# Forget biases from the score products into a per-pair mask tile

## The chip, the cores and the metric

One Trainium2 chip, one core. The metric is the device time of one execution in microseconds, lower is better. The profiled execution has a time of its own, and its trace's span runs from the first to the last instruction.

## What is computed

Two layers over 512 tokens of width 1024 in float32. Each layer has eight forget heads and eight dilated heads of 64. A forget head is softmax attention with a bias from cumulated log forget gates:

```python
c = jnp.cumsum(log_f, axis=1).transpose(0, 2, 1)
s = jnp.einsum('bqhd,bkhd->bhqk', q_i, k) * scale
s = s + c_i[..., :, None] - c[:, :, None, :]
s = jnp.where(causal, s, NEG)
prob = jax.nn.softmax(s, axis=-1)
```

The term of the query, c_i, is the same for a whole row and drops out of the softmax; the kernel adds the term of the key only. After attention come a SiLU gate, an output projection, and a gated per-layer embedding.

## The kernel before

Heads are handled in pairs of two, 64 rows each: pairs 0 to 3 of a layer are dilated, pairs 4 to 7 forget. Values are split into a high and a low part (fp32r), and a product of two split operands is three products on TensorE (hi x hi, hi x lo, lo x hi).

One pass p = 1 to 7 of the loop at L743 projects pair p for four token tiles (pj, L690), evacuates each tile (ev, L695: squares on ScalarE, sum `ms` on VectorE, power -0.5 `f` on GpSimd at L445, scaling `z` on VectorE at L458), and in between does the attention of the pair a = p - 1 and the value product of p - 2. Pair 7 is scored after the loop, in between parts of the output projection. TensorE's order is that of the program; the order on VectorE, ScalarE, GpSimd and SyncE is made by a scheduler when the program is built, and each engine then runs its order strictly in turn.

The scores are in att_s (L572). For four query tiles qt of 128 (3 first) and both heads j, products go into PSUM tiles of (qt+1) x 128 columns (at least 256): three for the split query and key and, for a forget pair, a fourth, whose stationary operand `low` is all ones and whose moving operand CB holds the cumulated log gates (L583 to L590). Rows 0 and 1 of each 64-row half of CB are the high and low part of the gates of one head, all other rows are zero. Scores carry a minus sign: the scale is -0.125 (L345), so the smallest is sought, and the exponential has scale -1. Then for each tile one VectorE instruction adds a mask (`mask_fox` or `mask_dil`, both in the constant tile `cst`) and takes the row minimum `mx` (L597), ScalarE makes the exponential and its sum (L599), VectorE the reciprocal (L600), GpSimd the scaling (L601).

The gates are cumulated once in a layer, in pass 4 (cumulate, L502): products with a triangle in `tri`, then C2, high parts in rows 0 to 7, low parts in rows 32 to 39. bias_rows (L518) copies four rows of C2 to CB for a pair, with four transfers on ScalarE's queue; it is called in pass 4 for pair 4 and after att_s in passes 5, 6, 7 for the next pair.

The probabilities are transposed by TensorE (att_tp, att_tp2, L608 and L614), split into `PT` (ScalarE L621, VectorE L622), and multiplied with the values. Weights come over SyncE's queue as `raw` (L115) and are split into whi (ScalarE L157) and wlo (VectorE L158). The gate of a pair is L482 (VectorE) and L483 (tanh on ScalarE); QQ and KK are the split query and key (L548 to L557).

Of the kernel before, what the change touches and what calls it, by code (L numbers as in the profile page):

```python
# [9 lines left out]
F32 = mybir.dt.float32  # L10
F32R = mybir.dt.float32r
I32 = mybir.dt.int32
AF = mybir.ActivationFunctionType
# [4 lines left out]
P = 128  # L18
# [37 lines left out]
def constants():  # L56
    i = np.arange(P)[:, None]
    j = np.arange(P)[None, :]
    ident = (i == j).astype(np.float32)
    causal = np.where(j <= i, 0.0, BIG)  # L60
    mf = np.concatenate([np.zeros((P, 3 * P)), causal], axis=1)
    blocks = []
    for b in (3, 2, 1, 0):
        dist = b * P + i - j
        c = (dist <= 128).astype(int) + (dist % 4 == 0) + (dist % 16 == 0)
        c = np.where(dist >= 0, c, 0)
        blocks.append(np.where(c > 0, -np.log(np.maximum(c, 1)), BIG))
    md = np.concatenate(blocks, axis=1)
    return np.ascontiguousarray(
        np.concatenate([ident, mf, md], axis=1).astype(np.float32))  # L70


NCST = P + 2 * S

# [127 lines left out]
def trunk(tc, ap):  # L202
# [3 lines left out]
    with ctx:  # L206
# [39 lines left out]
        ident = cst[:, 0:P]  # L246
        mask_fox = cst[:, P:P + S]
        mask_dil = cst[:, P + S:P + 2 * S]
        tri = cp.tile([P, 5 * P], F32R, name="tri")
        lf = cp.tile([P, NT, 40], F32R, name="lf")  # L250
# [18 lines left out]
        KK = [cp.tile([P, S], F32R, name=f"KK{i}") for i in range(2)]  # L269
        CB = cp.tile([P, S], F32R, name="CB")  # L270
        PT = [cp.tile([P, 13, P], F32R, name=f"PT{i}") for i in range(2)]
        for l in range(DEPTH):
            W.own[("pt", l)] = (QQ, KK)
        C2 = cp.tile([40, S], F32R, name="C2")
        fx = cp.tile([P, NT, 8], F32, name="fx")
        hs = dp.tile([NK, P, S], F32, name="hs")

        ang = cp.tile([P, NT, 8], F32, name="ang")
# [39 lines left out]
        V.memset(ones1, 1.0)  # L318
        G.memset(CB.bitcast(F32), 0.0)
        for j in range(2):  # L320
            G.memset(PT[j][:, 0].bitcast(F32), 0.0)
        G.memset(tri[:, 0:P].bitcast(F32), 0.0)
        G.memset(tri[:, 2 * P:].bitcast(F32), 1.0)
        G.memset(lf.bitcast(F32), 0.0)
# [12 lines left out]
        def scale_columns():  # L337
            V.scalar_tensor_tensor(tri[:, P:2 * P], mask_fox[:, 3 * P:], 1.0, ident, op0=ALU.min,
                                   op1=ALU.add)
# [162 lines left out]
        def cumulate():  # L502
# [3 lines left out]
            for t in range(NT):  # L506
                n = max(NT - t, 2) * P
                T.matmul(ps[0:40, S - n:], lf[:, t], tri[:, P:P + n] if t < 3 else tri[:, :n],
                         start=(t == 0), stop=(t == NT - 1))
            c = tp.tile([8, S], F32, tag="ob", name="c")  # L510
            A.activation(c, ps[32:40], AF.Copy)
            V.tensor_tensor(c, ps[0:8], c, op=ALU.add)
            A.activation(C2[0:8], c, AF.Copy)
            V.tensor_tensor(C2[32:40], c, C2[0:8].bitcast(F32), op=ALU.subtract)

        HALF = (slice(0, 64), slice(64, P))

        def bias_rows(a):  # L518

            for j in range(2):  # L520
                h = 2 * (a - NDIL) + j
                for i in range(2):
                    A.dma_start(CB[64 * j + i:64 * j + i + 1].bitcast(F32),  # L523
                                C2[32 * i + h:32 * i + h + 1].bitcast(F32))

# [46 lines left out]
        def att_s(a):  # L572
            fox = a >= NDIL
            mask = mask_fox if fox else mask_dil
            low = tri[:, 2 * P:3 * P]
            b3, b2, pm = pair(psS, "psS"), pair(psS, "psS"), pair(psM, "psM")
            tiles = {}
            for qt in (3, 2, 1, 0):
                n = (qt + 1) * P
                nt = max(qt + 1, 2)  # L580
                for j in range(2):
                    tiles[(j, qt)] = (pm[j][:, 256:], pm[j][:, :256], b2[j][:, :384], b3[j])[qt]
                for i, (x, y) in enumerate(((0, 0), (0, 1), (1, 0), (2, 2))[:4 if fox else 3]):  # L583
                    for j in range(2):
                        if x == 2:
                            lhs, rhs = low[HALF[j]], CB[HALF[j], :nt * P]
                        else:
                            lhs = QQ[x][HALF[j], qt * P:(qt + 1) * P]
                            rhs = keys(KK[y], j, nt)
                        T.matmul(tiles[(j, qt)], lhs, rhs, start=i == 0, stop=i == 2 + fox)  # L590
            for qt in (3, 2, 1, 0):
                n = (qt + 1) * P
                for j in range(2):
                    seg = pseg(j, qt)
                    mx = sp.tile([P, 1], F32, tag="mx", name="mx", bufs=8)
                    sm = sp.tile([P, 1], F32, tag="sm", name="sm", bufs=8)
                    V.tensor_tensor_reduce(seg, tiles[(j, qt)][:, :n], mask[:, S - n:], 1.0, 3e38,  # L597
                                           ALU.add, ALU.min, mx)
# [85 lines left out]
        for l in range(DEPTH):  # L684
# [58 lines left out]
            for p in range(1, NPAIR):  # L743
# [24 lines left out]
                if p > 1:  # L768
                    with behind("A", "V"):
                        W.pump()  # L770
                pj(p, 2)
                ev(p, 2)
# [35 lines left out]
            part(1, 3, 5)  # L808
            att_o(b, oo)
            att_s(a)  # L810
            PT1 = [x.rearrange("p k s -> p (k s)")[:, :13 * P].rearrange("p (a b) -> p a b", a=13)
# [155 lines left out]
```

## Time and profile before

| | |
|---|---|
| median of three runs | 712.31 us (711.62 to 1372.89) |
| profiled execution | 712.22 us, span 710.4 us |
| TensorE, matmul busy | 699.4 us, 98% |
| TensorE, weight loads busy | 618.4 us, 87% |
| VectorE busy | 501.8 us, 71% |
| ScalarE busy | 382.3 us, 54% |
| GpSimd busy | 182.9 us, 26% |
| granted clock of TensorE | 0.999 |
| read from HBM | 60.49 MB |

PE is TensorE, PEld its weight loads, DVE VectorE, ACT ScalarE, POOL GpSimd, SP SyncE. Times in rows are microseconds from the span's start unless marked ns. A bracket at a row's end says how long the engine sat idle ahead of it, and what ended that. L12 is a line of the kernel before. One run of the three took 1372.89 us; it plays no part below.

### The profile page before, as it was taken

The page shows a single profiled execution, that of the slowest core. Times are in us where ns is not written, and L with a number is a line of the kernel's source. Part 1 is how long each engine was busy: PE and PEld are TensorE (multiplying, and loading weights), DVE is VectorE, ACT ScalarE, POOL GpSimd, SP SyncE. Part 2 cuts the span into 40 slices and gives each one's busy share as a digit, 9 for nine tenths or more (in the row PEclk, how much of TensorE's full clock was granted, in tenths as well). Part 3 has the DMA queues.
Part 4 walks back from the last instruction along what each step waited for, and adds up shares of the span by engine and source line. Part 5 has one row for each costly group of instructions (what it writes and reads, how often), then busy time and mean ns, then how long its engine had stood idle before and what let it go on. Part 6 is the DMA issues. An engine that isn't in the chain of part 4 may idle for free.

```text
span 710.4 us, 12211 instructions
## 1 busy us (share of the span) xinstructions
PE 699.4 (98%) x4424; PEld 618.4 (87%) x4424; DVE 501.8 (71%) x1240; ACT 382.3 (54%) x809; POOL 182.9 (26%) x326
## 2 busy tenths in 40 slices
PE   9999999999999999999999999999999999999997
PEld 8999898989989878888899899998889897888886
DVE  7887787766767677838738687777767767694633
ACT  8575556555555756525425556555654656582310
POOL 7462643313131320000004533614131240200000
PEclk9999999999999999999999999999999999999999
DMA  8612131221212145424423022222222113353211
GB/s 289 194 32 68 57 99 50 86 68 54 90 57 88 36 139 150 157 83 156 139 69 119 8 90 60 84 67 70 73 65 86 60 61 119 105 163 118 89 44 45
DMA packets 23948, 65.53 MB, mean 92 GB/s; under 512 B 4817, under 2 KB 6097, under 8 KB 23889
## 3 DMA queue, kind: packets, MB, share of 16 engines
q1 hardware_dynamic: 22576, 64.68, 28.6%
q8 instruction: 35, 0.57, 0.3%
q10 hardware_dynamic: 1312, 0.08, 0.1%
q14 instruction: 25, 0.20, 0.1%
HBM read 60.49 MB, written 4.19 MB: 91 GB/s over the span
## 4 chain that ended last, share of the span: by engine, by line
PE 64%; DVE 17%; ACT 8%; issue 4%; POOL 4%; ACTq 2%; DMA 0%; POOLq 0%; DVEq 0%
PE psA L88 42%; PE psS L88 16%; DVE wlo L158 5%; PE psM L88 4%; POOL f L445 3%; DVE PT L622 3%; ACT U L599 3%; ACTq L523 2%; ACT PT L621 1%; DVE U L597 1%; DVE U L653 1%; ACT whi L157 1%; ACT sqh L483 1%; DVE V L452 1%; DVE ms L442 1%
## 5 line engine op out<-in xcount | busy, mean ns | idle before, releaser
L157 ACT ACTIVATE whi<-raw 128x1024 fp32r<-128x1024 f32 (+3 forms) x105 | 106.7, 1021 | 68.2 <-PE psA L88 51.7
L158 DVE TENSOR_TENSOR wlo<-raw,whi 128x1024 fp32r<-128x1024 f32 (+3 forms) x105 | 122.8, 1171 | 13.3 <-ACT whi L157 13.2
L88 PE MATMUL psA<-whi,X 128*128 128x384 f32 (+1 forms) x480 | 130.5, 341 | 0.0
L88 PE MATMUL psA<-whi,Y 128*128 128x384 f32 (+1 forms) x480 | 129.3, 341 | 0.2 <-DVE U L482 0.2
L445 POOL TENSOR_TENSOR f<-ms,mhalf 128x4 f32<-128x4 f32 x64 | 64.7, 1012 | 243.7 <-DVE ms L443 234.1
L88 PE MATMUL psA<-Y,whi 128*128 128x512 f32 (+1 forms) x320 | 96.6, 385 | 0.7 <-DVE sqh L863 0.5
L88 PE MATMUL psA<-X,whi 128*128 128x512 f32 x304 | 95.7, 396 | 0.0
L599 ACT ACTIVATE U<-U,mx 128x512 f32<-128x512 f32 (+3 forms) x128 | 70.6, 553 | 39.4 <-DVE mx L597 34.5
L88 PEld LDWEIGHTS psA<-whi,X 128*128 128x128 f32 x480 | 87.9, 188 | 1.8 <-ACT whi L157 0.5
L88 PEld LDWEIGHTS psA<-whi,Y 128*128 128x128 f32 x480 | 87.5, 188 | 1.4 <-issue 0.4
L88 PE MATMUL psA<-wlo,X 128*128 128x384 f32 (+1 forms) x240 | 81.8, 341 | 1.7 <-DVE wlo L158 1.7
L88 PE MATMUL psA<-wlo,Y 128*128 128x384 f32 (+1 forms) x240 | 81.3, 339 | 1.2 <-DVE wlo L158 1.2
L601 POOL TENSOR_SCALAR U<-U,sm 128x512 f32<-128x512 f32 (+3 forms) x128 | 65.8, 534 | 55.0 <-DVE sm L600 54.2
L88 PEld LDWEIGHTS psA<-Y,whi 128*128 128x128 f32 x320 | 58.4, 188 | 13.5 <-DVE sqh L863 1.2
L88 PEld LDWEIGHTS psA<-X,whi 128*128 128x128 f32 x304 | 56.5, 188 | 13.1 <-DVE sqh L863 0.4
L88 PE MATMUL psA<-Y,wlo 128*128 128x512 f32 (+1 forms) x160 | 61.3, 383 | 0.0
L88 PE MATMUL psA<-X,wlo 128*128 128x512 f32 x152 | 59.9, 394 | 0.0
L458 DVE TENSOR_TENSOR z<-psA,f 128x256 f32<-128x256 f32 x60 | 25.4, 423 | 45.9 <-POOL f L445 45.9
L622 DVE TENSOR_TENSOR PT<-psS,PT 128x512 fp32r<-128x512 f32 (+1 forms) x58 | 37.1, 673 | 19.1 <-ACT PT L621 19.1
L440 ACT ACTIVATE sq<-psA 128x256 f32<-128x256 f32 x56 | 21.3, 381 | 53.4 <-PE psA L88 45.8
L88 PEld LDWEIGHTS psA<-wlo,X 128*128 128x128 f32 x240 | 45.2, 188 | 3.2 <-DVE wlo L158 3.2
L88 PEld LDWEIGHTS psA<-wlo,Y 128*128 128x128 f32 x240 | 45.1, 188 | 2.0 <-DVE wlo L158 2.0
(190 smaller groups left out, 1232.5 us busy)
## 6 DMA issues: line engine op xcount, KB each, us to landing
raw<-in_wq_dram SPq DMA_DIRECT2D x28, 576.0 KB, 3.9
raw<-in_wg_dram SPq DMA_DIRECT2D x16, 512.0 KB, 3.4
raw<-in_wo_dram SPq DMA_DIRECT2D x16, 512.0 KB, 3.4
raw<-in_wpg_dram SPq DMA_DIRECT2D x16, 512.0 KB, 3.4
raw<-in_wq_dram SPq DMA_DIRECT2D x14, 384.0 KB, 3.3
U<-in_xT_dram SPq DMA_DIRECT2D x16, 256.0 KB, 3.9
raw<-in_wple_dram SPq DMA_DIRECT2D x4, 512.0 KB, 3.6
hs<-U SPq DMA_DIRECT2D x8, 256.0 KB, 3.2
```

What stands on the lines that cost most here:

```text
L88: return self.tc.keep_in_program_order(self.eng.matmul(*a, **k))
L157: self.nc.scalar.activation(hi, r, AF.Copy)
L158: eng.tensor_tensor(lo, r, hi.bitcast(F32), op=ALU.subtract)
L440: A.activation(sq, ps[:, :2 * P].rearrange("p (h d) -> p h d", h=4), AF.Square)
L442: V.tensor_reduce(ms, sq, axis=AX.X, op=ALU.add)
L445: G.tensor_tensor(f, ms, mhalf.to_broadcast([P, 4]), op=ALU.pow)
L452: V.scalar_tensor_tensor(v2[:, t, :, HD:P], vps, st["r"][:, t:t + 1], v2[:, t, :, 0:HD].bitcast(F32), op0=ALU.mult, op1=ALU.subtract)
L458: last["V"] = V.tensor_tensor(z, ps[:, :2 * P].rearrange("p (h d) -> p h d", h=4), f[:, :, None].to_broadcast([P, 4, HD]), op=ALU.mult)
L523: A.dma_start(CB[64 * j + i:64 * j + i + 1].bitcast(F32), C2[32 * i + h:32 * i + h + 1].bitcast(F32))
L599: A.activation(seg, seg, AF.Exp, bias=mx, scale=-1.0, accum_out=sm)
L601: G.tensor_scalar(seg, seg, sm, 1.0, op0=ALU.mult, op1=ALU.mult)
L622: last["V"] = V.tensor_tensor(lo, src, hi.bitcast(F32), op=ALU.subtract)
```

## The change

The fourth product goes, with `low`, CB and C2. In their place stands MF, a tile of 20 blocks of 128 x 128 in float32: for head j and query tile qt the blocks that fox_mask names hold what L597 adds. cumulate writes the cumulated gates c (8 heads x 512) to HBM (`cd`). For a pair, bias_rows issues eight transfers on SyncE's queue, each of which reads the first (qt+1) x 128 gates of one head from `cd` and writes them to all 128 partitions of MF. bias_causal adds the causal block to the diagonal blocks of one head in one VectorE instruction of 128 x 4 x 128, so twice for a pair. The constant tile holds one causal block in place of four blocks, and `tri` loses its block of zeros.

```diff
@@ constants
-    mf = np.concatenate([np.zeros((P, 3 * P)), causal], axis=1)
-        np.concatenate([ident, mf, md], axis=1).astype(np.float32))
-NCST = P + 2 * S
+        np.concatenate([ident, causal, md], axis=1).astype(np.float32))
+NCST = 2 * P + S
@@ trunk
-        mask_fox = cst[:, P:P + S]
-        mask_dil = cst[:, P + S:P + 2 * S]
-        tri = cp.tile([P, 5 * P], F32R, name="tri")
+        causal = cst[:, P:2 * P]
+        mask_dil = cst[:, 2 * P:]
+        tri = cp.tile([P, 4 * P], F32R, name="tri")
-        CB = cp.tile([P, S], F32R, name="CB")
+        MF = cp.tile([P, 20, P], F32, name="MF")
-        C2 = cp.tile([40, S], F32R, name="C2")
+        cd = dp.tile([8, S], F32, name="cd")
@@ cumulate
-                n = max(NT - t, 2) * P
-                T.matmul(ps[0:40, S - n:], lf[:, t], tri[:, P:P + n] if t < 3 else tri[:, :n],
-                         start=(t == 0), stop=(t == NT - 1))
+                n = (NT - t) * P
+                T.matmul(ps[0:40, S - n:], lf[:, t], tri[:, :n], start=(t == 0),
+                         stop=(t == NT - 1))
             c = tp.tile([8, S], F32, tag="ob", name="c")
             A.activation(c, ps[32:40], AF.Copy)
             V.tensor_tensor(c, ps[0:8], c, op=ALU.add)
-            A.activation(C2[0:8], c, AF.Copy)
-            V.tensor_tensor(C2[32:40], c, C2[0:8].bitcast(F32), op=ALU.subtract)
+            nc.sync.dma_start(cd, c)
@@ bias_rows
+        def fox_mask(j, qt):
+            x0 = 7 + 3 * qt if j == 0 else 12 - 4 * qt
+            return MF[:, x0:x0 + qt + 1].rearrange("p a b -> p (a b)")
+
         def bias_rows(a):
-            for j in range(2):
-                h = 2 * (a - NDIL) + j
-                for i in range(2):
-                    A.dma_start(CB[64 * j + i:64 * j + i + 1].bitcast(F32),
-                                C2[32 * i + h:32 * i + h + 1].bitcast(F32))
+            for qt in range(NT):
+                for j in range(2):
+                    h = 2 * (a - NDIL) + j
+                    n = (qt + 1) * P
+                    nc.sync.dma_start(fox_mask(j, qt), cd[h:h + 1, :n].to_broadcast([P, n]))
+
+        def bias_causal():
+            for x in (MF[:, 7:20:4], MF[:, 3:13:3]):
+                V.tensor_tensor(x, x, causal[:, None, :].to_broadcast([P, NT, P]), op=ALU.add)
@@ att_s
-                for i, (x, y) in enumerate(((0, 0), (0, 1), (1, 0), (2, 2))[:4 if fox else 3]):
+                for i, (x, y) in enumerate(((0, 0), (0, 1), (1, 0))):
                     for j in range(2):
-                        if x == 2:
-                            lhs, rhs = low[HALF[j]], CB[HALF[j], :nt * P]
-                        else:
-                            lhs = QQ[x][HALF[j], qt * P:(qt + 1) * P]
-                            rhs = keys(KK[y], j, nt)
-                        T.matmul(tiles[(j, qt)], lhs, rhs, start=i == 0, stop=i == 2 + fox)
+                        T.matmul(tiles[(j, qt)], QQ[x][HALF[j], qt * P:(qt + 1) * P],
+                                 keys(KK[y], j, nt), start=i == 0, stop=i == 2)
-                    V.tensor_tensor_reduce(seg, tiles[(j, qt)][:, :n], mask[:, S - n:], 1.0, 3e38,
+                    mask = fox_mask(j, qt) if fox else mask_dil[:, S - n:]
+                    V.tensor_tensor_reduce(seg, tiles[(j, qt)][:, :n], mask, 1.0, 3e38,
                                            ALU.add, ALU.min, mx)
@@ pass p, ahead of pj(p, 2)
+                if a >= NDIL:
+                    bias_causal()
@@ after the loop
             att_o(b, oo)
+            bias_causal()
             att_s(a)
```

The scheduler places what the program asks for elsewhere than the text does. In pass 5 of each layer, VectorE comes to the two additions for pair 4 behind KK: one ahead of two halves of PT, one between the sum of squares `ms` and its scaling. The additions for pairs 5, 6 and 7 it sets a good deal earlier than the program's text, right behind the attention of the pair before. VectorE's order at the end of att_s for pair 4, in pass 5, in the kernel before (L600 is the last reciprocals, L442, L452 and L443 the evacuation of the pass's last token tile, L158 a weight split, L482 the gate):

```order
L597 ISA U_92,mx<-psM,cst 128x128
L597 ISA mx 128x1
L600 RECIPROCAL sm<-sm 128x1 x4
L442 TENSOR_REDUCE ms<-sq 128x4
L452 SCALAR_TENSOR_TENSOR V_116<-psA,r,V_116 128x2x64
L443 TENSOR_SCALAR ms<-ms,E 128x4
L458 TENSOR_TENSOR z<-psA,f 128x256
L158 TENSOR_TENSOR wlo<-raw,whi 128x1152
L482 TENSOR_TENSOR U_94<-psA,Rh 128x512
```

and in the changed kernel, whose own line numbers its rows carry (L529 is the addition, L439, L449, L440, L455, L157 and L479 are L442, L452, L443, L458, L158 and L482 of before):

```order
L597 ISA U_92,mx<-psM,MF 128x128
L597 ISA mx 128x1
L600 RECIPROCAL sm<-sm 128x1 x4
L529 TENSOR_TENSOR MF<-MF,cst 128x4x128
L439 TENSOR_REDUCE ms<-sq 128x4
L449 SCALAR_TENSOR_TENSOR V_116<-psA,r,V_116 128x2x64
L440 TENSOR_SCALAR ms<-ms,E 128x4
L529 TENSOR_TENSOR MF<-MF,cst 128x4x128
L455 TENSOR_TENSOR z<-psA,f 128x256
L157 TENSOR_TENSOR wlo<-raw,whi 128x1152
L479 TENSOR_TENSOR U_94<-psA,Rh 128x512
```

The two additions for pair 5 now stand inside the evacuation of the last token tile, the first ahead of its reduction, the second ahead of its z. It is the same in passes 6 and 7.

VectorE's order where att_s of pair 4 begins, before (the first four rows evacuate token tile 2):

```order
L442 TENSOR_REDUCE ms<-sq 128x4
L452 SCALAR_TENSOR_TENSOR V_116<-psA,r,V_116 128x2x64
L443 TENSOR_SCALAR ms<-ms,E 128x4
L458 TENSOR_TENSOR z<-psA,f 128x256
L597 ISA U_88,mx<-psS,cst 128x512
L597 ISA mx 128x1
L597 ISA U_91,mx<-psS,cst 128x512
```

and in the changed kernel:

```order
L439 TENSOR_REDUCE ms<-sq 128x4
L449 SCALAR_TENSOR_TENSOR V_116<-psA,r,V_116 128x2x64
L440 TENSOR_SCALAR ms<-ms,E 128x4
L597 ISA U_88,mx<-psS,MF 128x512
L597 ISA mx 128x1
L455 TENSOR_TENSOR z<-psA,f 128x256
L597 ISA U_91,mx<-psS,MF 128x512
```

The first mask reduction has moved ahead of z.

SyncE's order from the transfer of c to the weights of pass 6 in the changed kernel (L510 writes `cd`, L525 is a transfer into MF, L114 a weight load; before, only the weight loads stood there):

```order
L114 DMA raw<-in_wq_dram 128x1152
L510 DMA cd<-c 8x512
L525 DMA MF<-cd 128x128 x2
L525 DMA MF<-cd 128x256 x2
L525 DMA MF<-cd 128x384 x2
L525 DMA MF<-cd 128x512 x2
L114 DMA raw<-in_wq_dram 128x1152
L114 DMA raw<-in_wq_dram 128x768
L114 DMA raw<-in_wg_dram 128x1024
L525 DMA MF<-cd 128x512 x2
L525 DMA MF<-cd 128x384 x2
L525 DMA MF<-cd 128x256
```

Each later group of eight has the widest first, and stands behind the gate's weights of its pass and ahead of the loads of the next.

## Rows read from the trace of the kernel before

**Rows 1.** Windows, one per step: length, busy time (instructions) by engine, clock, DMA
```profile
147.23:178.49 31.26, 30.68 (x222) 27.88 (x222) 21.59 (x59) 17.81 (x42) 8.15 (x12) 1.00 0.24 68
178.49:209.47 30.98, 30.59 (x221) 28.05 (x220) 22.52 (x61) 17.39 (x41) 8.15 (x12) 1.00 0.23 70
209.47:240.09 30.62, 30.42 (x222) 28.02 (x222) 21.56 (x58) 17.24 (x41) 8.36 (x14) 1.00 0.21 70
406.76:436.32 29.56, 29.56 (x213) 27.44 (x213) 22.60 (x64) 17.40 (x41) 13.96 (x24) 1.00 0.23 72
496.02:527.37 31.35, 30.77 (x222) 27.90 (x222) 21.37 (x58) 17.87 (x42) 8.15 (x12) 1.00 0.23 69
527.37:558.62 31.25, 30.72 (x221) 28.11 (x220) 22.74 (x61) 17.40 (x41) 8.16 (x13) 1.00 0.23 68
558.62:589.33 30.71, 30.48 (x221) 28.06 (x220) 22.24 (x60) 17.22 (x41) 8.44 (x14) 1.00 0.22 70
```

**Rows 2.** Timeline of TensorE (start, length, instruction): score blocks, forget and dilated
```profile
196.70 0.97 PE L88 MATMUL psS<-KK,QQ 64*128 64x512 f32 x6
...
199.48 0.45 PE L88 MATMUL psA<-whi,X 128*128 128x384 f32 x1
...
424.19 1.50 PE L88 MATMUL psS<-KK,QQ 64*128 64x512 f32 x12
...
426.33 0.44 PE L88 MATMUL psA<-whi,Y 128*128 128x384 f32 x1
```

**Rows 3.** Timeline: transfers and tanh in pass 4, a wait of TensorE in pass 6
```profile
147.44 2.52 ACTq L523 DMA_DIRECT2D CB<-C  x4
...
150.01 0.63 ACT L483 ACTIVATE sqh<-U 128x512 f32<-128x512 f32 x1 [2.60 <-issue]
...
185.94 0.44 PE L88 MATMUL psA<-wlo,X 128*128 128x384 f32 x1 [0.39 <-DVE wlo L158]
```

**Rows 4.** The page's part 4, the chain that ended last, by engine
```profile
PE 64%; DVE 17%; ACT 8%; issue 4%; POOL 4%; ACTq 2%; DMA 0%; POOLq 0%; DVEq 0%
```

**Rows 5.** Timeline of one forget step, VectorE, ScalarE and its queue
```profile
200.02 0.68 DVE L597 CUSTOM_DVE_ANT_0 U<-psS,cst 128x512 f32<-128x512 f32 x1
...
203.97 0.28 DVE L597 CUSTOM_DVE_ANT_0 U<-psM,cst 128x128 f32<-128x128 f32 x1
...
205.22 0.55 ACTq L523 DMA_DIRECT2D CB<-C  x1
...
205.81 0.60 ACTq L523 DMA_DIRECT2D CB<-C  x1
206.51 0.39 ACT L440 ACTIVATE sq<-psA 128x256 f32<-128x256 f32 x1 [0.99 <-ACT U L599]
206.93 0.42 DVE L442 TENSOR_REDUCE ms<-sq 128x4 f32<-128x256 f32 x1 [1.21 <-ACT sq L440]
...
208.94 0.42 DVE L458 TENSOR_TENSOR z<-psA,f 128x256 f32<-128x256 f32 x1 [1.20 <-POOL f L445]
```

**Rows 6.** Lines, shapes apart: a 128x512 addition on VectorE
```profile
L387 DVE TENSOR_TENSOR acc<-acc,sqh 128x512 f32<-128x512 f32 x28 | 19.3, 688 | 0.0
```

**Rows 7.** Timeline of a dilated step: VectorE's addition beside GpSimd
```profile
423.25 1.35 DVE L158 TENSOR_TENSOR wlo<-raw,whi 128x1152 fp32r<-128x1152 f32 x1
423.42 1.29 POOL L463 TENSOR_TENSOR tm<-z,Sg 128x32 f32<-128x32 f32 x1 [0.54 <-DVE z L458]
...
427.68 0.25 POOL L463 TENSOR_TENSOR tm<-z,Sg 128x32 f32<-128x32 f32 x1 [0.54 <-DVE z L458]
```

**Rows 8.** DMA issues: out<-in queue xcount, KB each, median us to landing
```profile
CB<-C ACTq DMA_DIRECT2D x32, 2.0 KB, 1.7
out_dram<-U SPq DMA_DIRECT2D x2, 128.0 KB, 1.7
gr<-in_qkg_dram SPq DMA_DIRECT2D x2, 16.0 KB, 3.9
```

**Rows 9.** Timeline of ScalarE in pass 7 of layer 0
```profile
237.78 0.38 ACT L440 ACTIVATE sq<-psA 128x256 f32<-128x256 f32 x1 [1.71 <-issue]
```

More of the change, by code (lines that the diff above doesn't have):

```diff
@@ L318, in trunk @@
         V.memset(ones1, 1.0)
-        G.memset(CB.bitcast(F32), 0.0)
         for j in range(2):
             G.memset(PT[j][:, 0].bitcast(F32), 0.0)
-        G.memset(tri[:, 0:P].bitcast(F32), 0.0)
-        G.memset(tri[:, 2 * P:].bitcast(F32), 1.0)
+        G.memset(tri[:, P:].bitcast(F32), 1.0)
         G.memset(lf.bitcast(F32), 0.0)
@@ L337, in scale_columns @@
         def scale_columns():
-            V.scalar_tensor_tensor(tri[:, P:2 * P], mask_fox[:, 3 * P:], 1.0, ident, op0=ALU.min,
+            V.scalar_tensor_tensor(tri[:, 0:P], causal, 1.0, ident, op0=ALU.min,
                                    op1=ALU.add)
@@ L573, in att_s @@
             fox = a >= NDIL
-            mask = mask_fox if fox else mask_dil
-            low = tri[:, 2 * P:3 * P]
             b3, b2, pm = pair(psS, "psS"), pair(psS, "psS"), pair(psM, "psM")
```

## The prediction

> **What bounds the kernel now.** I read the steps first. A step runs from one pass's first block of transposes on TensorE to the next pass's. In [rows 1] a step whose scores belong to a dilated pair takes 29.56 us with TensorE busy throughout: such a step is TensorE-bound. The six steps that compute forget scores (three in each layer) take 30.62 to 31.35 us, 186.17 in all, against 6 x 29.56 = 177.36 at the dilated pace: 8.81 us more. The reader is to see that TensorE is busy for less than those spans.
>
> The fourth product explains part of it. The score block of a forget pair lasts from 196.70 to 199.48, 2.78 us; that of a dilated pair from 424.19 to 426.33, 2.14 us [rows 2]. So the product costs 0.64 us of TensorE per pair, 3.84 us in the six steps, and 1.28 us in the two pairs scored after the last pass, 5.12 us in all. The remaining 8.81 - 3.84 = 4.97 us of the six steps is TensorE waiting; [rows 3] end with one such wait, at 185.94, for a weight half (wlo) that VectorE makes late.
>
> Why VectorE is late is in the chain of waits, of which only 64% lies on TensorE [rows 4], and in the timeline of one step [rows 5]. The three products of its first block end at 196.70 + 0.97 = 197.67 [rows 2], but the first mask reduction starts at 200.02, because it stands in VectorE's order behind z, which waits for GpSimd's pow as the next z does at 208.94. Then follow eight reductions and eight exponentials; ScalarE, behind the last exponential, issues two transfers (0.55 and 0.60 us); the square comes at 206.51, its reduction on VectorE at 206.93, then GpSimd's pow, and z at 208.94. From there the weight split, the gate and the transposed probabilities follow without slack until the wait of [rows 3]. **The fourth product is not on this chain**: its end is covered by z. A forget step is as long as the chain, and taking work from TensorE alone lengthens TensorE's wait. What the change does to the chain therefore decides.
>
> **The change part by part.** The sum is made against the profiled execution's 712.2 us (span 710.4); the median of the runs shown is 712.31, so the two can be read as one.
>
> Fourth product: -0.64 us of TensorE per pair. In the six steps I count nothing for it by itself, since the chain hides it; with the cover gone it is worth the whole 0.64. After the last pass TensorE works through output-projection parts while the probabilities are made, so there it counts between 0 and 0.64; I take 0.6 per layer, nearer TensorE's side as the parts leave it little idle.
>
> First forget pass (p = 4) of each layer: the two casts of C2 and four transfers leave ScalarE. The transfers take ScalarE 2.52 us from 147.44 on, and the gate's tanh waits 2.60 us for them [rows 3]. What that step loses beyond product and pace is 31.26 - 29.56 - 0.64 = 1.06 us, the most that can come back. Against it stand two additions on VectorE in pass 5, each as long as a 128x512 addition, 0.69 us [rows 6]: one ahead of the second half of PT, which has room, one between two instructions that GpSimd's pow waits for. The new chain c to HBM and back (eight transfers behind one another on SyncE) starts at about 147.4, and ahead of the first addition VectorE has eight instructions of about the size of [rows 6], 8 x 0.69 = 5.5 us of work: room for two landings one after the other of under 3 us each. I take -0.7 per layer, between 0 and -1.06.
>
> Passes 5, 6, 7 of each layer, six times. Four things change on the chain of [rows 5]:
> (a) Two late transfers leave ScalarE: the square could follow the last exponential, about 1.1 us sooner (0.55 + 0.60; 205.4 in place of 206.51).
> (b) The first mask reduction now stands ahead of z and uses VectorE's wait for pow: the later seven come some 0.7 us sooner, and so do the exponentials.
> (c) The first addition for the next pair now stands right behind the last reciprocal and ahead of the reduction of squares. It waits for four transfers into MF, and those can be issued only when this pair's reductions have read MF. The last of the four follows the seventh reduction, which ended at 203.97 + 0.28 = 204.25 and by (b) ends near 203.5. With a time to landing of L the addition starts at 203.5 + L and the reduction of squares behind it at 203.5 + L + 0.69, against 206.93 now. Everything in VectorE's queue behind it (reduction, V, ms, z, the weight split, the gate) waits with it.
> (d) The second addition starts just ahead of GpSimd's pow. In [rows 7] a GpSimd operation of 0.25 us that meets a VectorE addition of two SBUF operands takes 1.29 us, until that addition ends. The pow itself was never met so (bounds: 0 and the 0.69 of the addition); I take 0.55, since the row that shows such a meeting shows a full wait.
> The shift of z is then 203.5 + L + 0.69 - 206.93 + 0.55 = L - 2.2 us.
>
> L is not shown for this transfer (one HBM row of 512 to 2048 bytes copied to 128 partitions). The nearest rows [rows 8]: 1.7 us for 2 KB and for 128 KB, and 3.9 us for a row broadcast to 128 partitions (gr) in the crowded first microseconds. The last transfer that counts is 64 KB and the queue is otherwise idle then, so I take 2.0, near the lower end: shift -0.2 us, with ends -0.5 (L = 1.7) and +1.7 (L = 3.9). Times six: -1.2, between -3.0 and +10.2.
>
> One term stands alone: in layer 0, pass 7, the transfers held the square back to 237.78, a wait of 1.71 us, not 0.99 [rows 5, 9]. That falls away: -0.7, once.
>
> Nothing is charged for bytes: 8 x 1.3 MB more is read, beside weight loads that are issued in good time. SyncE's order puts the eight transfers ahead of weight loads that are issued a step later anyway. In layer 0 the instructions of log_forget also come a little earlier in VectorE's and ScalarE's orders, in passes 1 and 2; TensorE does not depend on them before pass 4, and I count nothing.
>
> Sum: 2 x (-0.7 - 0.6) - 1.2 - 0.7 = -4.5 us; 712.2 - 4.5 = **707.7 us**.
>
> Two rules of the Trainium skill bear on (c) and (d), and the sum does without them. [Rows 7] show GpSimd held to the end of a VectorE addition; the page SBUF — State Buffer (SBUF: two separate sides) calls the port that VectorE's second SBUF input shares with GpSimd an exclusive lock, held for a whole instruction. By that rule (d) costs its 0.55, as charged; without it the sum would be 3.3 us lower, 704.4. [Rows 8] show what a wait right behind an issue costs here; the page DMA: Bandwidth & Descriptors (Rules for kernel authors) says to issue early, compute, and wait late. The order in (c) does the opposite of that, which is the second rival below.
>
> **The rivals.**
> 1. *TensorE becomes the bound of the forget steps too*: landing and pow hide, the chain gets shorter by (a) and (b), 1.8 us, less one addition, enough to cover TensorE's waits. Then all of 8.81 + 1.28 = 10.1 us comes back: 702.1 us. For it: TensorE is busy 98% and its waits are short. Against it: for 8.81 / 6 = 1.47 us per step, L - 2.2 has to fall to -1.47, which with (d) free still wants an L of 1.3 us, and no row shows one.
> 2. *The MF transfers land late, slower than before*: VectorE's in-order queue stands at the first addition in passes 5 to 7. The total of 2 x (-0.7 - 0.6) - 0.7 + 6 x (L - 2.2) passes zero at L = 2.75 us; at gr's 3.9 us it is +6.9: 719.1 us. For it: gr is the only row of this shape, and all 128 readers want one HBM row. Against it: gr lands in the crowded first microseconds, the MF transfers on an idle queue.
> 3. *The wait only changes its owner*: shift of z about 0.2 to 0.7 us, gains and new waits cancel: 710.1 to 713 us.
>
> **How the numbers follow.** Forecast (L of 1.7 to 2.4 and (d) of 0.2 to 0.55: 703.8 to 710.1 us): 0.5. Rival 1 (701 to 703.8): 0.13. Rival 3: 0.17. Rival 2: 0.2, of which 0.03 lies beyond 2%. The range that leaves out no more than 2 in 10 goes from 702 to 717; the forecast's own is 703.8 to 710.1. A measurement of this kernel can tell about 2%, 14 us, from no change. The floor of rival 1 is 1.4% below the present, so faster by over 2% gets 0.01; slower by over 2% needs L of about 5.1 us (14.2 + 3.3 = 17.5 us over six steps is a shift of 2.9), 0.03; within 2% 0.96.
>
> **What would show it.** Right: forget steps of about 30.3 to 30.6 us in passes 5 to 7, TensorE still waiting there for wlo, VectorE idle ahead of the first addition until MF lands, about 2 us after issue; the tanh of pass 4 no longer held. If the steps come down to 29.6 us, rival 1 holds. If the first addition starts after 207 on the scale of [rows 5], rival 2. If the pow behind the second addition takes 1.0 us with no delay, (d) is wrong. The forecast is wrong if dilated steps change by more than 0.1 us, for then something other than these waits moved.

## The result and the profile after

The changed kernel takes 729.29 us (median of four runs, 728.95 to 730.33) against 712.12 us of the kernel before on the same chip: ratio 1.0246, 95% interval 1.0226 to 1.0266. It is slower, and outside the range of 702 to 717. One run of the kernel before, 1372.89 us, counts in that median and is left out of the ratio.

The page's first lines of the changed kernel, busy time (share of the span) xinstructions, and the chain that ended last:

```profile
span 727.0 us, 12149 instructions
PE 701.6 (97%) x4360; PEld 621.2 (85%) x4360; DVE 509.3 (70%) x1254; ACT 379.6 (52%) x807; POOL 183.6 (25%) x324
...
PE 68%; DVE 14%; DMA 7%; POOL 4%; ACT 3%; issue 3%; SPq 1%; DVEq 0%; POOLq 0%; ACTq 0%
```

Against [rows 4], ScalarE and its queue have a smaller part of the chain (8% and 2% are now 3% and 0%) and DMA has come in with 7%. TensorE has 64 products fewer and yet is busy 2 us longer. The windows by step, as in [rows 1], the dilated step first, show where the time lies:

```profile
413.83:443.39 29.56, 29.56 (x213) 27.44 (x212) 22.61 (x64) 17.39 (x41) 13.97 (x24) 1.00 0.23 72
146.73:181.37 34.64, 31.32 (x214) 29.03 (x214) 22.61 (x61) 17.38 (x41) 7.39 (x12) 0.95 0.42 138
181.37:213.04 31.67, 30.26 (x213) 27.55 (x213) 22.38 (x59) 17.16 (x41) 8.20 (x12) 1.00 0.36 109
213.04:246.49 33.45, 31.51 (x214) 29.07 (x214) 23.98 (x65) 17.07 (x41) 8.89 (x15) 0.95 0.33 103
503.10:539.04 35.94, 32.22 (x213) 29.84 (x213) 22.32 (x61) 17.38 (x41) 7.21 (x12) 0.91 0.47 132
539.04:570.56 31.52, 30.13 (x214) 27.57 (x214) 23.12 (x60) 17.16 (x41) 8.07 (x12) 1.00 0.42 110
570.56:602.93 32.37, 30.28 (x214) 27.55 (x214) 22.24 (x60) 16.94 (x41) 8.74 (x14) 1.00 0.34 106
```

That dilated step is unchanged at 29.56 us. The first forget step of each layer is the worst (34.64 and 35.94 us, 31.26 and 31.35 before), and in three steps the granted clock is under 1.00, which it was in none before. The stretches behind the third forget steps, in which pair 7 is scored, are longer too: 23.64 and 25.25 us (246.49 to 270.13 and 602.93 to 628.18), 22.99 and 22.18 before. One dilated step is shorter, the first of layer 0: 29.51 us (56.66 to 86.17), 30.06 before. What VectorE waited for, in the view of waits (total, times, longest):

```profile
DVE MF L529 <- DMA MF<-cd: 27.1, 9, 4.8
...
PE psS L87 <- DVE PT L622: 7.3, 3, 3.7
PE psA L87 <- DVE U L479: 5.9, 6, 1.0
PE psM L90 <- DVE z L455: 3.5, 4, 1.6
```

The additions (L529) wait 27.1 us for transfers into MF, and TensorE then waits for what stands behind them in VectorE's order: the probabilities PT, the gate U, z. Two of the nine waits are for pair 4 (4.35 and 4.75 us); the others are for pairs 5 to 7. The timeline of VectorE in the step that [rows 5] showed, last reductions to z:

```profile
206.88 0.29 DVE L597 CUSTOM_DVE_ANT_0 U<-psM,MF 128x128 f32<-128x128 f32 x1
...
207.16 0.27 DVE L597 CUSTOM_DVE_ANT_0 U<-psM,MF 128x128 f32<-128x128 f32 x1
...
208.82 0.16 DVE L600 RECIPROCAL sm<-sm 128x1 f32<-128x1 f32 x1 [0.22 <-ACT U L599]
212.14 0.69 DVE L529 TENSOR_TENSOR MF<-MF,cst 128x512 f32<-128x512 f32 x1 [3.16 <-DMA MF<-cd]
212.75 0.41 DVE L439 TENSOR_REDUCE ms<-sq 128x4 f32<-128x256 f32 x1
...
213.47 0.69 DVE L529 TENSOR_TENSOR MF<-MF,cst 128x512 f32<-128x512 f32 x1
215.06 0.42 DVE L455 TENSOR_TENSOR z<-psA,f 128x256 f32<-128x256 f32 x1 [0.91 <-POOL f L442]
```

and of ScalarE, GpSimd, SyncE's queue and TensorE beside it:

```profile
208.69 0.36 ACT L437 ACTIVATE sq<-psA 128x256 f32<-128x256 f32 x1
...
213.71 1.32 POOL L442 TENSOR_TENSOR f<-ms,mhalf 128x4 f32<-128x4 f32 x1 [4.10 <-DVE ms L440]
...
203.34 5.71 SPq L525 DMA_DIRECT2D MF<-cd  x8
...
217.50 0.41 PE L87 MATMUL psA<-whi,X 128*128 128x384 f32 x1 [1.03 <-DVE U L479]
```

ScalarE's square follows the last exponential at 208.69 with no idle time, as (a) of the prediction had it. VectorE is done with the reciprocals at 208.98 and stands until 212.14. The seventh reduction ended at 206.88 + 0.29 = 207.17, so the "L" of the prediction is 212.14 - 207.17 = 4.97 us here, not 2.0; read alike at all six places it is 4.23 to 5.84. The pow behind takes 1.32 us beside the second addition.

Pass 4 to 5 is the place that the prediction had thought covered. SyncE's queue, VectorE and TensorE of the changed kernel there:

```profile
146.30 0.35 SPq L510 DMA_DIRECT2D cd<-c  x1
149.29 4.00 SPq L525 DMA_DIRECT2D MF<-cd  x8
...
152.91 0.87 DVE L561 SCALAR_TENSOR_TENSOR KK<-psM,gq,KK 128x256 fp32r<-128x256 f32 x2
158.12 0.69 DVE L529 TENSOR_TENSOR MF<-MF,cst 128x512 f32<-128x512 f32 x1 [4.35 <-DMA MF<-cd]
158.73 1.28 DVE L622 TENSOR_TENSOR PT<-psS,PT 128x512 fp32r<-128x512 f32 x2
...
155.95 0.80 PE L87 MATMUL psS<-PT,V 128*128 128x512 f32 x4
160.07 1.27 PE L87 MATMUL psS<-PT,V 128*128 128x512 f32 x4 [3.32 <-DVE PT L622]
161.14 0.52 PE L87 MATMUL psA<-whi,X 128*128 128x384 f32 x1
161.46 0.52 PE L87 MATMUL psA<-wlo,X 128*128 128x384 f32 x1
161.78 0.84 PE L87 MATMUL psA<-whi,X 128*128 128x384 f32 x2
```

The write to HBM takes 2.99 us until the first read is issued, the eight issues take 4.00 us, and the transfer issued seventh, of 256 KB, takes 5.6 us from issue to landing (152.38 to 158.00). The addition starts at 158.12. TensorE stands for 3.32 us, and the same four products then take 1.27 us in place of 0.80. The windows there (columns as above; the seventh number is the granted clock):

```profile
155.00:160.00 5.00, 1.75 (x11) 1.50 (x9) 1.88 (x4) 0.00 (x0) 0.00 (x0) 1.00 0.66 245
160.41:163.83 3.42, 3.42 (x13) 3.42 (x12) 2.49 (x7) 1.91 (x3) 1.01 (x1) 0.50 0.00 0
164.00:167.00 3.00, 3.00 (x19) 3.00 (x18) 2.51 (x6) 1.81 (x4) 0.28 (x1) 1.00 0.48 131
218.44:221.85 3.41, 3.41 (x12) 3.41 (x12) 3.31 (x7) 3.23 (x8) 0.00 (x0) 0.50 0.28 106
515.40:522.23 6.83, 5.38 (x17) 5.28 (x18) 5.83 (x12) 1.90 (x3) 1.01 (x1) 0.50 0.15 55
607.56:610.97 3.41, 3.00 (x7) 2.45 (x8) 2.23 (x5) 3.12 (x7) 0.00 (x0) 0.50 0.47 154
```

After a stretch in which TensorE was busy 1.75 of 5 us the granted clock is 0.50, the lower of its two levels (1.2 of 2.4 GHz), and it is back at 1.00 from 164: 13 products in 3.42 us, then 19 in 3. The last three rows are the other such stretches in this trace, each behind waits of TensorE for VectorE: 17.07 us in all at 0.50, TensorE busy for 15.21 of them.

### The profile page after: what moved, and what is told of

The parts are those of the page before. It is cut to its first block, busy times and chain, and to the rows that moved or that the text cites. A ratio compares the mean times of both kernels' runs of the same rounds, so it can differ in the third digit from the quotient of the medians.

```text
span 727.0 us, 12149 instructions
## 1 busy us (share of the span) xinstructions
PE 701.6 (97%) x4360; PEld 621.2 (85%) x4360; DVE 509.3 (70%) x1254; ACT 379.6 (52%) x807; POOL 183.6 (25%) x324
## 3 DMA queue, kind: packets, MB, share of 16 engines
HBM read 70.78 MB, written 4.23 MB: 103 GB/s over the span
## 4 chain that ended last, share of the span: by engine, by line
PE 68%; DVE 14%; DMA 7%; POOL 4%; ACT 3%; issue 3%; SPq 1%; DVEq 0%; POOLq 0%; ACTq 0%
PE psA L87 46%; PE psS L87 17%; DMA MF<-cd 6%; PE psM L87 4%; DVE wlo L157 4%; POOL f L442 3%; DVE PT L622 2%; ACT U L599 1%; DVE z L455 1%; DVE U L597 1%; SPq L525 1%; DMA cd<-c 1%; DVE ms L439 1%; PE psS L90 1%; PE psM L90 1%
## 5 line engine op out<-in xcount | busy, mean ns | idle before, releaser
L87 PE MATMUL psA<-whi,X 128*128 128x384 f32 (+1 forms) x480 | 132.8, 346 | 2.1 <-DVE U L479 2.1
L442 POOL TENSOR_TENSOR f<-ms,mhalf 128x4 f32<-128x4 f32 x64 | 67.5, 1056 | 265.0 <-DVE ms L440 255.2
L157 DVE TENSOR_TENSOR wlo<-raw,whi 128x1024 fp32r<-128x1024 f32 (+3 forms) x105 | 122.9, 1172 | 13.6 <-ACT whi L156 13.3
L87 PEld LDWEIGHTS psA<-whi,X 128*128 128x128 f32 x480 | 89.9, 193 | 4.0 <-issue 2.5
L455 DVE TENSOR_TENSOR z<-psA,f 128x256 f32<-128x256 f32 x60 | 25.4, 423 | 40.3 <-POOL f L442 40.3
L87 PE MATMUL psS<-PT,V 128*128 128x512 f32 x240 | 45.8, 332 | 7.9 <-DVE PT L622 7.3
L87 PEld LDWEIGHTS psS<-PT,V 128*128 128x128 f32 x240 | 40.6, 191 | 12.7 <-DVE PT L622 7.9
L480 ACT ACTIVATE sqh<-U 128x512 f32<-128x512 f32 x16 | 10.1, 632 | 73.6 <-DVE U L479 73.6
```

Source lines behind the costliest of these rows:

```text
L87: return self.tc.keep_in_program_order(self.eng.matmul(*a, **k))
L157: eng.tensor_tensor(lo, r, hi.bitcast(F32), op=ALU.subtract)
L442: G.tensor_tensor(f, ms, mhalf.to_broadcast([P, 4]), op=ALU.pow)
L455: last["V"] = V.tensor_tensor(z, ps[:, :2 * P].rearrange("p (h d) -> p h d", h=4), f[:, :, None].to_broadcast([P, 4, HD]), op=ALU.mult)
L480: A.activation(th, gt, AF.Tanh)
```

## The experiments

The theory after the result: the loss is VectorE's queue, which stands at additions that the scheduler set early until the transfers land. Rivals: the 10.3 MB more of traffic (70.78 MB read in place of 60.49), the additions' own time and their meeting with GpSimd, or one bad place that sets off the rest. Each run is set against the kernel before on its own chip, whose medians there lie between 712.12 and 713.18 us; two runs on different chips can therefore be compared to about 1 us.

**Late additions.** Same work, the two additions held behind z of the second token tile of the pass that uses them:

```diff
                 if a >= NDIL:
-                    bias_causal()
+                    with behind("V"):
+                        bias_causal()
@@ after the loop
-            bias_causal()
+            with behind("V"):
+                bias_causal()
```

> The changed kernel with one thing moved: the two additions of a pair stand on VectorE in the pass that uses them, behind the scaling of the second token tile, some 13 us after MF's transfers were issued, and no longer right behind the last reciprocal of the pair before. Bytes, transfers and additions are the same. Theory (VectorE's queue stood at the first addition until the transfers had landed, and everything behind it stood too): no addition waits for a transfer, and the time falls from 729.3 to 702 to 708 us. Rival (the 10.3 MB more of traffic, or the additions' own time on VectorE and the port, slow the kernel): 722 to 729 us, and the loss shows at other waits.

701.43 us, ratio to the kernel before 0.9839 (0.9824 to 0.9854), the granted clock 0.999. Its three forget steps of layer 0:

```profile
146.50:176.03 29.53, 29.53 (x214) 27.45 (x214) 22.39 (x61) 17.39 (x41) 8.15 (x12) 1.00 0.51 160
176.03:205.92 29.89, 29.82 (x215) 27.46 (x214) 23.36 (x62) 17.28 (x41) 8.14 (x12) 1.00 0.36 116
205.92:235.69 29.77, 29.77 (x214) 27.43 (x214) 23.25 (x62) 17.07 (x41) 8.44 (x14) 1.00 0.38 115
```

TensorE is busy nearly throughout and the steps are within 0.33 us of the dilated pace. All bytes still move; no addition waits for a transfer. So 27.9 us of the changed kernel's time hang on where sixteen instructions stand.

**No additions; no transfers either; the transfers of before on another queue.**

```diff
@@ no additions: both calls of bias_causal() left out
@@ no bias: no additions, bias_rows() moves nothing, cd written in layer 0 only, MF made once on GpSimd
+            G.memset(MF, 0.0)
+            for x in (MF[:, 7:20:4], MF[:, 3:13:3]):
+                G.tensor_tensor(x, x, causal[:, None, :].to_broadcast([P, NT, P]), op=ALU.add)
@@ kernel before, CB on SyncE's queue
-                    A.dma_start(CB[64 * j + i:64 * j + i + 1].bitcast(F32),
+                    nc.sync.dma_start(CB[64 * j + i:64 * j + i + 1].bitcast(F32),
```

> The changed kernel without the additions: the scores of forget pairs get the gates, but no causal mask (this part of the computation is left out). The transfers are all there. Theory: nothing on VectorE waits for them before the reductions of the next pass, 701 to 706 us, within 2 us of the kernel with late additions. Rival (traffic and contention): 720 us or more. If it stands more than 3 us below the late additions, the additions have a price of their own.

699.06 us, 0.9803 (0.9789 to 0.9818).

> The changed kernel without the transfers and the additions of every pair: MF is filled once with zeros and the causal blocks, so forget scores lack the cumulated gates (this part is left out). It is the floor of what leaving out the product and ScalarE's transfers can give. Expected by the theory: 700 to 705 us, and the kernel without additions at most 2 us above it. By the rival of traffic it stands 15 us or more below that kernel.

700.31 us, 0.9819 (0.9805 to 0.9834). It has less to do than the one without additions but fills MF on GpSimd at the start: its first block of transposes comes at 86.92 us against 85.74, and from there on the steps of the two agree to 0.1 us. So the traffic by itself costs nothing that can be seen here, and the rival of traffic falls.

> The kernel before with one edit: its four small transfers of a pair into CB are issued on SyncE's queue in place of ScalarE's. Product, CB and masks stay. It takes the first term of the prediction alone (two late transfers off ScalarE, 1.1 us in six steps, 0.7 once, and up to 1.06 in pass 4 of both layers): expected 3 to 8 us below the kernel before, 704 to 709 us. If it stays at 712, the transfers on ScalarE were hidden.

706.75 us, 0.9911 (0.9894 to 0.9927). In the kernel before the forget steps take between 30.62 and 31.35 us; here they take 30.65 and 30.69 (the first of each layer) and 30.16 to 30.22 (the other four). The latter are the dilated 29.56 plus the product's 0.64: with ScalarE's transfers gone, TensorE is the bound and the product is no longer hidden. Leaving out the product and the bias rows as well (700.31) takes another 6.4 us.

**Which place costs what.** One of the two places put late, the other left as the changed kernel has it (the diff of late additions, with `a == NDIL` for pair 4 or `a > NDIL` and the call after the loop for pairs 5 to 7). In the first of the two the scheduler set the second addition of pair 5 two instructions later than in the changed kernel, behind the weight split:

> The changed kernel with the additions of pair 4 alone put late, as in the kernel with all additions late; those of pairs 5, 6 and 7 stand where the changed kernel has them. By the steps of the two traces (34.64 and 35.94 us against 29.53 twice) the pair-4 place costs 5.1 + 6.4 = 11.5 us. Theory: the two places add up, so 729.3 - 11.5 = 718 us, give or take 2. Rival 1 (the loss is all in the six places the prediction spoke of): 727 to 730. Rival 2 (a first long wait with the lower clock behind it sets off the later ones): under 710.

718.01 us, 1.0070 (1.0053 to 1.0087).

> The reverse: additions of pairs 5, 6 and 7 late, those of pair 4 where the changed kernel has them. Theory (places add up): 701.4 + 11.5 = 713 us, give or take 2. Rival 1: 701 to 704. Rival 2: over 720.

712.96 us, 1.0003 (0.9993 to 1.0012). The places add up: pair 4 costs 712.96 - 701.43 = 11.5 us, pairs 5 to 7 cost 718.01 - 701.43 = 16.6, together 28.1 against the 27.9 lost. Both rivals are out.

**The place without the wait.** The kernel without additions, with additions of constants, into a tile that nothing reads there, at the places in VectorE's order that the additions for pairs 5 to 7 had:

```diff
+        def decoy(k):
+            with tc.issue_after(last[k].ins):
+                V.tensor_tensor(acc.rearrange("p (a b) -> p a b", a=NT),
+                                mask_dil.rearrange("p (a b) -> p a b", a=NT),
+                                causal[:, None, :].to_broadcast([P, NT, P]), op=ALU.add)
```

> The kernel without MF additions (scores lack the causal mask), with two additions of the same size on constant tiles put back at the very places on VectorE where the changed kernel has those for pairs 5, 6 and 7: they take their 0.69 us and meet GpSimd, but have no transfer to wait for. Theory (the wait is the loss): 699 to 704 us, that is at most 5 us over the 699.1 without additions, and about 0.5 us of delay in the pow behind the second one. Rival (the place itself, ahead of the sum of squares and beside the pow, costs what was lost): 706 to 716 us.

699.10 us, 0.9809 (0.9795 to 0.9824): not distinguishable from no additions. VectorE and GpSimd in the step of layer 0 that answers to the one above:

```profile
203.06 0.69 DVE L516 TENSOR_TENSOR acc<-cst 128x512 f32<-128x512 f32 x1
204.66 0.42 DVE L455 TENSOR_TENSOR z<-psA,f 128x256 f32<-128x256 f32 x1 [0.91 <-POOL f L442]
...
203.30 1.32 POOL L442 TENSOR_TENSOR f<-ms,mhalf 128x4 f32<-128x4 f32 x1 [0.28 <-DVE ms L440]
```

The pow is 0.3 us longer than the 1.01 it takes alone (0.14 in two of the six places), and that costs nothing that can be seen here. What was lost is the wait.

**Why the transfers land late.** Number, size and place of the transfers kept, but 128 or 16 rows of HBM to read from in place of one; and the two last transfers of a pair alone:

```diff
@@ 128 rows (all heads' gates); with 16 rows a head the write is this one and each row is read by eight partitions
-        cd = dp.tile([8, S], F32, name="cd")
+        cd = dp.tile([P, S], F32, name="cd")
-            nc.sync.dma_start(cd, c)
+            nc.sync.dma_start(cd.rearrange('(h k) s -> h k s', h=8), c[:, None, :].to_broadcast([8, 16, S]))
-                    nc.sync.dma_start(fox_mask(j, qt), cd[h:h + 1, :n].to_broadcast([P, n]))
+                    nc.sync.dma_start(fox_mask(j, qt), cd[:, :n])
@@ the last two alone, on the kernel with pair 4 late
-            for qt in range(NT):
+            for qt in range(1):
```

> The changed kernel with another source of MF's transfers: the gates are written to HBM sixteen times, and partition p of a transfer reads row p of that table, so 128 readers have 128 rows and no longer one (the heads' gates are mixed up by that, an altered part of the computation). Number, size and place of the transfers stay. If the one row that all partitions read makes the landing slow, the median landing falls from 4.2 us to about 2 to 3 and the first additions wait 1 to 2 us less, 712 to 722 us. If it is the queue of eight transfers and their 128 rows each, landing stays within 0.4 of 4.2 us and the time at 726 to 732 (pair 4 may shift by a microsecond, the write to HBM being 16 times as large).

707.96 us, 0.9932 (0.9917 to 0.9947). The scheduler moved pair 4's additions late by itself here and left the others where that kernel with pair 4 late has them, so this stands against its 718.01: 10 us less.

> The changed kernel with each head's gates in sixteen rows of HBM, each read by eight partitions (what is computed is the same). The order of VectorE is that of the kernel with pair 4 late (718.0 us, one row) and of the one with 128 rows (708.0). If it is the number of readers of one row that makes the landing slow, eight readers are near one: 707 to 711 us and a median landing of 3.3 to 3.6. If distinct places of any number are not the point (mixing of heads, or the larger write), it stays near 718.

710.15 us, 0.9966 (0.9954 to 0.9978). VectorE's order is that of the 128 rows.

> The kernel with pair 4 late (718.0 us), and of a pair's eight transfers only the two of 64 KB that are issued last, each from one row of HBM (the gates are left out of the other blocks of MF, which keep their causal blocks). In that kernel these two land 4.5 us after issue, with 128 readers of one row and the rest of the pair's transfers ahead of them; with 16 or 128 rows they land in 2.9 to 3.0. If one row is slow because what is ahead piles up (each reader waits for those before), the lone transfers land in 2.6 to 3.1 us, the waits of the additions fall from 16.3 to some 7, and the time to 706 to 710. If a single transfer of one row is slow by itself, they still take over 4 us and the time stays at 715 to 718.

709.54 us, 0.9956 (0.9939 to 0.9972). Here the scheduler set each second addition of pairs 5 to 7 right behind the first, so that not only the landing differs from the kernel with pair 4 late. The DMA issues (count, size, median us to landing), first of the kernel with pair 4 late:

```profile
MF<-cd SPq DMA_DIRECT2D x16, 256.0 KB, 3.5
MF<-cd SPq DMA_DIRECT2D x16, 192.0 KB, 3.7
MF<-cd SPq DMA_DIRECT2D x16, 128.0 KB, 4.7
MF<-cd SPq DMA_DIRECT2D x16, 64.0 KB, 4.5
```

with 128 rows:

```profile
MF<-cd SPq DMA_DIRECT2D x16, 256.0 KB, 3.4
MF<-cd SPq DMA_DIRECT2D x16, 192.0 KB, 3.5
MF<-cd SPq DMA_DIRECT2D x16, 128.0 KB, 2.8
MF<-cd SPq DMA_DIRECT2D x16, 64.0 KB, 2.9
```

and with the 64 KB transfers alone, each from one row:

```profile
MF<-cd SPq DMA_DIRECT2D x16, 64.0 KB, 2.9
```

These medians are over all pairs. For pairs 5 to 7 the large transfers are issued first, and they land alike from one row and from 128; the small ones, issued behind them, gain 1.6 to 1.9 us. One row alone is not slow either: a transfer of 64 KB from one row lands in 2.9 us when nothing of the pair but the other 64 KB is ahead of it. It is the place in the queue and not the size: for pair 4 the order is the other way round, and there, with pair 4 late, the 64 KB transfers from one row land 2.8 to 3.1 us after issue and the 256 KB ones behind them 5.9 and 6.0, against 3.0 to 3.6 where they come first, and 3.7 to 4.3 behind the small ones from 128 rows. So it takes both, 128 readers of one row and other such transfers ahead. The additions' wait falls with it, and the time follows:

| additions of pairs 5 to 7 early, pair 4 late | waits for MF, us | time, us |
|---|---|---|
| one row, eight transfers | 16.3 | 718.01 |
| 16 rows a head | 8.9 | 710.15 |
| one row, two transfers | 6.8 | 709.54 |
| 128 rows | 6.1 | 707.96 |
| no wait (all late) | 0 | 701.43 |

From the first row to the fourth that is 10.2 us of waiting for 10.05 us of time. With 16 rows an issue takes SyncE 0.52 to 0.60 us in place of 0.32 to 0.43 for most, so the wait is longer there than with 128 rows though the landing is nearly the same. What the chip does inside, with several transfers that want one row, no run shows.

**A better place.** The late additions still cost 701.43 - 699.06 = 2.4 us. Two other places for them, with pair 4 late as before in the first (in the second the lines that set the place are left out here):

```diff
@@ behind the gate, pairs 5 to 7
                 rest = gate_evac(p, gps)
+                if p > NDIL:
+                    with behind("V"):
+                        bias_causal()
@@ on GpSimd, behind the pow of the first token tile
-                V.tensor_tensor(x, x, causal[:, None, :].to_broadcast([P, NT, P]), op=ALU.add)
+                G.tensor_tensor(x, x, causal[:, None, :].to_broadcast([P, NT, P]), op=ALU.add)
```

> The kernel with late additions, but those for pairs 5, 6 and 7 stand on VectorE behind the gate of the pass before (U, 0.68 us), where the trace of the late kernel shows VectorE idle for 1.18 us until ScalarE's first half of PT; pair 4's stay late. The late kernel lies 2.4 us over the one without additions (701.4 against 699.1). Theory (the additions then sit in idle time, and MF has landed some 4.6 us behind the last reduction, just before): 699 to 701 us. Rival (the landing is still out there, or the PT behind them is late): 702 to 708.

700.10 us, 0.9823 (0.9810 to 0.9837).

> The additions on GpSimd in place of VectorE, behind the pow of the next pass's first token tile, where the trace shows GpSimd idle for over 4 us. If an addition of 128x512 takes GpSimd about 1 us and hinders VectorE little: 699 to 701 us. Rival (an operation of two SBUF operands on GpSimd holds up VectorE's of the same kind, as the pow is held up the other way): 702 to 706, with VectorE's additions and splits beside it longer than in the late kernel.

699.51 us, 0.9820 (0.9807 to 0.9834). An addition takes GpSimd 1.28 to 1.30 us in eight cases and 1.75 to 2.29 in the other eight, not about 1. It does touch VectorE: the weight split that runs beside it takes 1.49 us, not 1.23 as in the kernel with late additions.

```profile
187.25 3.54 POOL L529 TENSOR_TENSOR MF<-MF,cst 128x512 f32<-128x512 f32 x2
...
188.14 1.49 DVE L157 TENSOR_TENSOR wlo<-raw,whi 128x1024 fp32r<-128x1024 f32 x1 [0.26 <-ACT whi L156]
```

In this kernel the additions for pairs 4 and 7 still wait for MF (1.18, 0.64, 1.04 and 1.62 us), but on GpSimd, where nothing stands behind them that TensorE needs soon: the steps there take 29.5 us. Both stand 1.8% below the kernel before; the intervals overlap, so neither is shown to be the faster.

## Why the prediction was wrong

**The step that failed is L in (c).** The mechanism was named: VectorE in order, the first addition behind the last reciprocal, everything behind it late with it. It stood as the second rival, with its price of 6 us per us of L, and it was given 0.03 beyond 2%. The size was taken from the wrong rows. Of [rows 8], CB moves from SBUF to SBUF and the output goes to HBM; the only read from HBM among them, gr, took 3.9. The DMA view of the kernel before has a nearer row, reads from HBM of tiles that the program itself had written there, and no kind of read from HBM has a lower median in it:

```profile
U<-hs SPq DMA_DIRECT2D x8, 256.0 KB, 2.8
```

MF's transfers are reads from HBM too, and even alone they land in 2.9 us, which is over the 2.75 at which the prediction's own sum turns. The reason given for the low end, that the queue is otherwise idle then, overlooked the pair's own transfers: with the larger ones ahead, on one row, the 64 KB transfers of pairs 5 to 7 land 4.2 to 5.6 us after issue in the changed kernel. From the seventh reduction to the addition it came to 4.97 us, beyond the upper bound of 3.9 as well.

**The price per us of L held, the rest of the sum did not.** Read at the six places, L is 4.84 us in the mean with pair 4 late and 3.18 with 128 rows; six times the difference is 10.0 us, and the times differ by 10.05. But with these L the prediction's sum gives 724.7 and 714.8 us, where 718.01 and 707.96 were measured. It is about 7 us too high at both, so the other terms gave more than was charged; the smaller (d), the tails and the first step of layer 0 (all below) are part of it, and the rest stays open. With L = 4.97 the sum gives 725.5 us, near the 729.29 measured, but by luck: these 7 us too many stand in for most of what pair 4 cost.

**Pass 4 to 5 was costed as two landings and a gain of 0.7 us a layer; it cost 11.5 us over both layers.** The range given, 0 to -1.06, had no room for a loss. The two landings of "under 3 us each" left out the issuing and the queue: the write took 2.99, but eight issues took SyncE 4.00 us, and the last transfers took 5.6 us to land, not 3. From cd's issue to the addition were 11.8 us (146.30 to 158.12), not 6. Room for them there was not: VectorE had finished KK at 153.78 and stood 4.35 us.

**The clock was not in the sum at all.** The changed kernel's 4360 products are busy for 701.6 us, those of the kernel with late additions, the same products, for 691.5. Some 10 us of the 27.9 are thus slower or stretched products and not idle time. The four stretches at 0.50 above account for most of that: half of the 15.21 us in which TensorE was busy there is 7.6 us, an estimate of what the clock took. With late additions no such stretch is left before the last 2 us of the span.

**(a) and (b) were right.** With CB on SyncE's queue the six steps lose 4.0 us, and the two stretches behind them, the tails in which pair 7 is scored, lose 2.0 more, which the 8.81 us that the prediction read from the steps alone do not contain. The square follows the last exponential at once, and the tanh of pass 4 starts at 147.56 us without the 2.60 us of [rows 3]. For (b): from the last `ms` instruction ahead of the reductions (L443, now L440) to the second reduction are 1.75 us in the step shown (202.49 to 204.24), 2.35 before (198.28 to 200.63), so 0.6 us less where 0.7 was expected.

**(d) was right in kind.** The pow beside the second addition took 1.32 us, not 1.01, in four of the six places: 0.3, not the 0.55 that was charged. In one it met the addition 0.2 us sooner and took 1.53, and in one it started ahead of the addition and took 1.02. The Trainium skill's page SBUF — State Buffer (SBUF: two separate sides) has the two engines share a port; that the trace agrees shows in 1.32 beside 1.01, and the GpSimd additions show it the other way, with the weight split's 1.49 beside 1.23.

**The product**: its 0.64 us in the tail came as charged (21.61 to 20.98 us with and without it, in layer 0). In the steps rival 1 was nearer than the forecast: with no wait at the additions TensorE is the bound and all that rival's 10.1 us and some more come back (701.43 against 702.1). Its condition, an L of 1.3 us, was wrong: it rests on the place of the additions, not on L. The sign named for rival 2, a first addition that starts after 207 on the scale of [rows 5], is what the trace shows: 212.14 less the 2.88 us by which this step begins later (181.37 against 178.49) is 209.26. The sign named against the whole forecast came too: the first dilated step of layer 0 changed by 0.55 us (30.06 to 29.51), where the earlier places of log_forget's instructions had been counted as nothing; which of the edits did it no run shows.

## What to carry to other kernels

Where a change adds a wait on a transfer to an engine that runs in order, ask first what stands behind the waiting instruction, and price the landing with rows of the same direction and with the issues and the change's own transfers in front of it. Put the consumer next to its use and not next to its earliest possible start: here that alone turned 2.5% slower into 1.6% faster with the same work; the Trainium skill's page DMA: Bandwidth & Descriptors (Rules for kernel authors) has the rule, wait late, and the runs agree with those 27.9 us. A chain off TensorE that is only just longer than TensorE's work hides gains: the product's 0.64 us a step show only once ScalarE's transfers are out of the chain (30.16 to 30.22 us in four of six steps with it, 29.51 to 29.57 without). What leaving out the product alone would have given no run shows.

## What the runs showed of the hardware that was not expected

- Several transfers in a row that each copy one HBM row to 128 partitions: 64 KB issued behind the larger ones land in 4.2 to 5.6 us, 256 KB issued behind the smaller ones in 5.6 to 5.9 (the changed kernel). With 16 or 128 distinct rows the 64 KB land in 2.9 to 3.0 in the median, and so they do from one row with no larger ones in the queue.
- After 3.32 us in which TensorE stood, its granted clock was 0.50 for 3.4 us, and 128x384 products started 0.32 us apart (161.14, 161.46, 161.78) in place of 0.17.
- An addition of 128x512 with two SBUF operands took GpSimd 1.28 to 2.29 us against VectorE's 0.69.
